# Neighbourhood attention: the reciprocal softmax sums of thirteen steps go through DRAM in place of a TensorE transpose

## The chip, the cores and the metric

The program runs on one core of one Trainium2 chip. The metric is the device time of one execution in microseconds (us), taken as the median of several runs. TensorE does matrix products and transposes into PSUM, VectorE and ScalarE do elementwise work, GpSimd moves small pieces and issues some transfers, and SyncE (SP) issues most transfers to and from DRAM. In the profile TensorE is PE (its weight loads are PEld), VectorE is DVE, ScalarE is ACT, GpSimd is POOL, and SPq is the queue of instructions of SyncE.

## The reference, cut to what matters

The reference is a network of two layers on 256 tokens of width 1024 with 256 context tokens, all in float32. The first layer mixes tokens with a retention, the second with a neighbourhood attention; an MLP follows each. The change lies in the neighbourhood attention (32 heads of 32 columns; the image is 4 rows of 64 columns). Every query sees the tokens in a window of its columns in all four rows, with a bias for each relative position, and all 256 context tokens:

```python
s_loc = jnp.einsum('bqhd,bikhd->bhqik', q_r, k_band).astype(jnp.float32) + bias
s_ctx = jnp.einsum('bqhd,blhd->bhql', q_r, k_c).astype(jnp.float32)
s = jnp.concatenate([s_loc.reshape(b, nh, GRID_W, band), s_ctx], axis=-1)
prob = jax.nn.softmax(s, axis=-1).astype(v.dtype)
p_loc = prob[..., :band].reshape(b, nh, GRID_W, kh, GRID_W)
return (jnp.einsum('bhqik,bikhd->bqhd', p_loc, v_band)
        + jnp.einsum('bhql,blhd->bqhd', prob[..., band:], v_c))
```

The kernel takes the exponentials first, multiplies them with the values, and divides by the sum of the exponentials at the end. The change concerns how the reciprocals of these sums reach the place where they are multiplied in.

## The kernel before, in words

The attention is cut into 16 steps, numbered n. Step n handles four heads (group `g = n // 2`) and half of the columns (`qt = n % 2`), that is 128 queries. A step consists of these functions:

- `scores(n)`: TensorE multiplies queries and keys into four PSUM banks, one for each head (`pqk`).
- `soften(n)`: for each head VectorE adds the bias and takes the minimum (the scores are kept negated), and ScalarE takes the exponential and adds up each row on the way. The sums of the four heads stand in a tile `sums[n]` of 128 queries x 4 heads, one of three buffers.
- `gather(n)`: GpSimd copies a few columns together and issues the loads of the bias of step n + 2.
- `invert(n)`: VectorE takes the reciprocal of the 4 sums of each query in place and copies it 32 times side by side into `rr` (128 queries x 128 columns: 32 equal columns for each head).
- `flip(n)`: TensorE transposes the exponentials in blocks of 128 x 128 into four PSUM banks (`ppt`, thirteen transposes), and ScalarE and VectorE copy them to SBUF (`pt`). At its end `flip_sums(n)` has TensorE transpose `rr` into the right part of a half of the bank `pav`, so that partition 32 j + d holds head j's reciprocals along the queries.
- `turned(n)`: ScalarE copies this transposed block from PSUM to the SBUF tile `rts[n]` (`rt` in the profile, one of two buffers).
- `attend(n)`: TensorE multiplies the transposed exponentials with the values into `pav`; VectorE multiplies the result with `rts[n]`; ScalarE and VectorE split the product into a high and a low part (`oTh`, `oTl`) for the output projection.

The steps are written out in a software pipeline. In iteration n of the loop over `STEPS` (n from 0 to 12) the scores and the softmax are those of step n + 2, the transposes those of step n + 1, and the attention product that of step n. The tuple of an iteration says how many units of weights are fetched and split at three places (`early` and `late` on either side of the softmax, `last` ahead of `attend`), and which projections run ahead of `flip` and behind `attend`. Between the steps stand the projections that make the keys, queries and values of later steps, and the first output projections. Before the loop stand `scores`, `soften` and `invert` of steps 0 and 1 and `flip(0)`; after the loop stand the last steps, by hand.

The order of the work on TensorE, ScalarE and VectorE is the order of the program text in this part of the kernel (an edge pins each instruction behind the one before it on its engine). On SP and GpSimd it is not: a planner that goes through the program at compile time puts their instructions in an order that respects all dependencies, and each of these queues then runs strictly in its order on the chip. SP issues the loads of weights: `fetch` loads a unit of 512 KB into one of four buffers (`raw`), ScalarE makes a rounded copy (`hi`), and VectorE the rest (`lo`, in `lows`); only when `lo` is made is the buffer free for the transfer four units later. Most helpers record their operations in one place, so that nearly every row of the profile has the line L84; rows are told apart by their tiles.

Of the kernel before, what the change touches and what calls it, by code (L numbers as in the profile page):

```python
# [10 lines left out]
F32 = mybir.dt.float32  # L11
# [6 lines left out]
P = 128  # L18
# [9 lines left out]
HD = 32  # L28
# [76 lines left out]
def kernel(  # L105
# [23 lines left out]
    pe, act, dve, pool, sp = (  # L129
        InOrder(tc, getattr(nc, e), e in PIN)  # L130
        for e in ("tensor", "scalar", "vector", "gpsimd", "sync")
    )
# [3 lines left out]
    smp = ec(tc.tile_pool(name="smp", bufs=4))  # L136
# [6 lines left out]
    dram = ec(tc.tile_pool(name="dram", bufs=1, space=DRAM))  # L143
# [8 lines left out]
    def nm(s):  # L152
        uid[0] += 1
        return f"{s}_{uid[0]}"

    def bank(s="ps"):
        return psp.tile([P, 512], F32, tag="ps", name=nm(s))
# [8 lines left out]
    def tsl(t):  # L166
        return slice(t * P, (t + 1) * P)
# [87 lines left out]
    def fetch(n, in_scratch=False, at=None):  # L255

        for src, k, ncol in specs[len(units) : len(units) + max(n, 0)]:
            raw = rawp.tile([P, k, ncol], F32, tag="raw", name=nm("raw"))
            sp.dma_start(out=raw[:], in_=src.rearrange("(k p) n -> p k n", p=P))
            if in_scratch or len(units) in scratch_units:  # L260
                hi, lo = Rows([scr("hi", F32R) for _ in range(k)]), Rows([scr("lo", F32R) for _ in range(k)])
                for i in range(k):
                    act.copy(out=hi[:, i, :], in_=raw[:, i, :])
                    pending.append((lo[:, i, :], raw[:, i, :], hi[:, i, :]))
                units.append((hi, lo))
                continue
            if at is None:
                hi = hip.tile([P, k, ncol], F32R, tag="hi", name=nm("hi"))
                lo = lop.tile([P, k, ncol], F32R, tag="lo", name=nm("lo"))
            else:  # L270
                both = slot(at, [P, 2, k, ncol], F32R, "hilo")
                hi, lo = both[:, 0], both[:, 1]
            act.copy(out=hi[:], in_=raw[:])
            pending.append((lo[:], raw[:], hi[:]))
            units.append((hi, lo))

    def lows(n=100, eng=None):
        for lo, raw, hi in pending[:n]:
            (eng or dve).tensor_sub(out=lo, in0=raw, in1=hi.bitcast(F32))
        del pending[:n]  # L280
# [591 lines left out]
    def part_v(k, a, b):  # L872
# [8 lines left out]
        out=lgn[:, 0], in_=ret_decay[0].rearrange("(o d) h -> o (d h)", o=1).broadcast_to([P, 8])  # L881
# [118 lines left out]
    for h in range(RH):  # L1000
# [102 lines left out]
        for t in range(4):  # L1103
            po = bank("po")
            scs = list(range(4)) if t < 2 else [2, 3]
            for i, sc in enumerate(scs):
# [9 lines left out]
                out=on, in0=po[:], scalar1=mv[:, 0:1], scalar2=r[:], op0=ALU.subtract, op1=ALU.mult  # L1116
# [312 lines left out]
    NS = 16  # L1429
# [70 lines left out]
    def v_part(half, t):  # L1500
        if t == 0:
            vu[0] = take(4, 0)
        ps = bank("pnv")
        for k in range(KC):
            wh, wl = vu[0][k // 2]
            mm3(ps[:], hs(k, t * P, (t + 1) * P), (wh[:, k % 2, :], wl[:, k % 2, :]), k == 0, k == KC - 1)
        act.copy(out=vtile(t, half), in_=ps[:])
# [28 lines left out]
    sums, rrs, Es, pts, pss = {}, {}, {}, {}, {}  # L1536

    def scores(n):

        g, qt = n // 2, n % 2  # L1540
        pss[n] = [bank("pqk") for _ in range(4)]
        q, k = q_of(g), kTs[g // 2][:, g % 2]
        for i, (a, b) in enumerate(((0, 0), (0, 1), (1, 0))):
            for j in range(4):
                js = slice(32 * j, 32 * j + 32)
                pe.matmul(
                    pss[n][j][:], lhsT=q[js, a, tsl(qt)], rhs=k[js, b, :], start=(i == 0), stop=(i == 2),
                    tile_position=(32 * j, 0),
                )

    def soften(n):

        mn = smp.tile([P, 4], F32, tag="mn", name=nm("mn"), bufs=3)
        sm = sums[n] = smp.tile([P, 4], F32, tag="sums", name=nm("sums"), bufs=3)
        for j in range(4):
            s = Es[n, j] = scr("s")
            dve.tensor_tensor_reduce(
                out=s[:].rearrange("p (a t) -> p a t", a=2),
                in0=pss[n][j][:].rearrange("p (a t) -> p a t", a=2),
                in1=bias_ap(n, j),  # L1560
                scale=1.0,
                scalar=3.0e38,
                op0=ALU.add,
                op1=ALU.min,
                accum_out=mn[:, j : j + 1],
            )
            act.activation(
                out=s[:], in_=s[:], func=AF.Exp, scale=-1.0, bias=mn[:, j : j + 1], accum_out=sm[:, j : j + 1]
            )
# [4 lines left out]
    def av_half(n):  # L1574
        return av[0][:, 256 * (n % 2) : 256 * (n % 2) + 256]

    def invert(n):

        rr = rrs[n] = smp.tile([P, 4, HD], F32, tag="rr", name=nm("rr"), bufs=1)
        dve.reciprocal(out=sums[n][:], in_=sums[n][:])  # L1580
        dve.tensor_copy(out=rr[:], in_=sums[n][:].unsqueeze(2).broadcast_to([P, 4, HD]))


# [4 lines left out]
    def pt_at(n, i):  # L1588
        return turns[n % 2][:, tsl(i)]

    def gather(n):

        o = 0 if n % 2 else P
        c0 = 24 if n % 2 else 0
        for j in range(4):
            pool.tensor_copy(
                out=pt_at(n, RAW)[:, 32 * j : 32 * j + 32].rearrange("p (r c) -> p r c", r=4),
                in_=Es[n, j][:, o : o + P].rearrange("p (r c) -> p r c", r=4)[:, :, c0 : c0 + 8],
            )
        if n + 2 < NS:  # L1600
            load_bias(n + 2)

    def flip(n, sums_too=True):
        for j in range(4):
            pp = bank("ppt")
            for i, kc in enumerate((n % 2, 2, 3)):
                pe.transpose(pp[:, tsl(i)], Es[n, j][:, tsl(kc)], ident)
            w = 3 * P
            if j == 3:
                pe.transpose(pp[:, tsl(3)], pt_at(n, RAW), ident)  # L1610
                w = 4 * P
            (dve.tensor_copy if j % 2 else act.copy)(
                out=turns[n % 2][:, 3 * j * P : 3 * j * P + w], in_=pp[:, :w]
            )
        if sums_too:
            flip_sums(n)

    def flip_sums(n):
        pe.transpose(av_half(n)[:, P:], rrs[n][:].rearrange("p h d -> p (h d)"), ident)

    oTs = [None]
    rts = {}

    def turned(n):

        rts[n] = smp.tile([P, P], F32, tag="rt", name=nm("rt"), bufs=2)
        act.copy(out=rts[n][:], in_=av_half(n)[:, P:])
# [30 lines left out]
    def rest_mm(half):  # L1658

        pr = bank("pnv")  # L1660
        sels = scr("sel")
        for qt in range(2):
            sel = sels[:, 32 * qt : 32 * qt + 32]
            pool.tensor_copy(
                out=sel.rearrange("p (r c) -> p r c", r=4),
                in_=ident.rearrange("p (r c) -> p r c", r=4)[:, :, 24 * qt : 24 * qt + 8],
            )
            v = vtile(1 - qt, half).rearrange("p (g j d) -> p j g d", g=4, j=4)
            for j in range(4):
                pe.matmul(  # L1670
                    pr[32 * j : 32 * j + 32, tsl(qt)], lhsT=sel, rhs=v[:, j], start=True, stop=True,
                    tile_position=(0, 32 * j),
                )
        return pr
# [96 lines left out]
    soften(1)  # L1771
    v_part(0, 1)
    invert(0)
    flip(0)
    rests = rest_mm(0)
    residual(1, xns[1], gb, dve)
    v_part(0, 2)
    rest_evac(rests)
    invert(1)
    v_part(0, 3)  # L1780

# [34 lines left out]
    def run(fs):  # L1816
        for f in fs:
            f()

    for n, (early, late, last, before, after) in enumerate(STEPS):  # L1820
        gather(n + 1)
        turned(n)
        fetch(early)
        lows(early)
        scores(n + 2)
        soften(n + 2)
        fetch(late)
        lows(late)
        run(before)
        flip(n + 1)  # L1830
        invert(n + 2)
        fetch(last)
        attend(n)
        run(after)

        lows(100 if n < len(STEPS) - 2 else len(STEPS) - 1 - n)


    n = NS - 1
    gather(n - 1)  # L1840
    turned(n - 2)
    flip(n - 1, False)
    fetch(1)
    attend(n - 2)
# [368 lines left out]
```

## Time and profile before

| | us |
|---|---|
| median of 3 runs (lowest to highest) | 1177.96 (1176.31 to 1180.05) |
| the profiled execution, its own time | 1176.32 |
| its span, first to last instruction | 1174.4 |
| TensorE busy in the span | 1161.8 |
| VectorE busy in the span | 848.4 |
| ScalarE busy in the span | 481.1 |
| GpSimd busy in the span | 235.1 |

The steps of the neighbourhood attention lie from about 819 us to 978 us after the start of the span. A row of the timeline names the start, the duration, the engine, the operation, the tile written and, behind the arrow, the tiles read, then how many instructions the row merges. What stands in brackets is the idle time of the engine ahead of it and what ended it. Matmuls overlap one another on TensorE, so that the distance from one start to the next, and not the duration, is what one costs.

### The profile page before, as it was taken

To read this page: it belongs to the slowest core of one execution; us is meant where nothing else is said; L and a number is where in the kernel's file an instruction comes from. 1 tells how busy PE (TensorE), PEld (TensorE's weight loads), DVE (VectorE), ACT (ScalarE), POOL (GpSimd) and SP (SyncE) were. 2 spreads that over 40 slices of the span, in tenths; PEclk is the share of its full clock that TensorE was granted. 3 is DMA by queue.
4 is the path that set the end of the run, shared out by engine and by line. 5 is a ranking of instruction groups with operands and counts; after the bars stand their busy time and mean duration, and the time that the engine had idled before them with its cause. 6 is when DMAs were issued, how large, how long until landed. Compare 5 with 4: busy or idle time off the path is not lost.

```text
span 1174.4 us, 17544 instructions
## 1 busy us (share of the span) xinstructions
PE 1161.8 (99%) x6687; PEld 980.7 (84%) x6687; DVE 848.4 (72%) x1361; ACT 481.1 (41%) x819; POOL 235.1 (20%) x418
## 2 busy tenths in 40 slices
PE   9999999999999999999999999999999999999997
PEld 6788888888888889888888888879778878999886
DVE  3786687777898787757777675578577589877456
ACT  3643332222323246441212333137466666756341
POOL 0102001010220241770312001223443430000001
PEclk9999999999999999999999999999999999999999
DMA  9943552544355426756556665646344335766760
GB/s 275 277 130 105 162 187 96 156 153 144 112 178 177 140 65 220 181 113 215 177 184 198 211 200 179 197 157 202 81 136 144 107 113 160 214 206 205 237 215 36
DMA packets 140115, 195.10 MB, mean 166 GB/s; under 512 B 9936, under 2 KB 81136, under 8 KB 140032
## 3 DMA queue, kind: packets, MB, share of 16 engines
q1 hardware_dynamic: 131904, 182.03, 49.8%
q0 software_dynamic: 6976, 9.39, 3.8%
q10 hardware_dynamic: 1152, 2.56, 0.7%
q8 instruction: 52, 0.85, 0.3%
q14 instruction: 31, 0.25, 0.1%
HBM read 189.12 MB, written 5.75 MB: 166 GB/s over the span
## 4 chain that ended last, share of the span: by engine, by line
PE 74%; DMA 12%; DVE 8%; issue 3%; ACT 2%; POOL 0%; DVEq 0%; ACTq 0%
PE p L84 23%; DMA rawa<-in_ada_w_dram 11%; PE pq L84 8%; PE pv L84 8%; PE pw L84 7%; PE pg L84 7%; PE pn L84 4%; DVE acc L84 4%; PE pnv L84 4%; PE po L84 3%; DVE lo L84 3%; PE pnw L84 1%; PE ppt L84 1%; PE pS L84 1%; PE pav L84 1%
## 5 line engine op out<-in xcount | busy, mean ns | idle before, releaser
L84 ACT CAST hi<-raw 128x1024 fp32r<-128x1024 f32 (+2 forms) x228 | 231.9, 1032 | 306.7 <-PE p L84 114.2
L84 DVE TENSOR_TENSOR lo<-raw,hi 128x1024 fp32r<-128x1024 f32 (+2 forms) x228 | 272.6, 1210 | 101.3 <-ACT hi L84 101.1
L84 PE MATMUL p<-hi,hid 128*128 128x512 f32 (+1 forms) x780 | 238.2, 386 | 0.0
L84 PEld LDWEIGHTS p<-hi,hid 128*128 128x128 f32 x780 | 145.7, 188 | 29.3
L84 PE MATMUL p<-hTl,hi 128*128 128x256 f32 (+1 forms) x512 | 165.9, 326 | 0.0
L84 PE MATMUL p<-hTh,lo 128*128 128x256 f32 (+1 forms) x512 | 165.9, 326 | 0.0
L84 PE MATMUL p<-hTh,hi 128*128 128x256 f32 (+1 forms) x512 | 162.6, 327 | 0.0
L84 PE MATMUL p<-lo,hid 128*128 128x512 f32 (+1 forms) x390 | 150.8, 387 | 2.1 <-DVE lo L84 2.1
L84 DVE SCALAR_TENSOR_TENSOR acc<-rawa,scol,acc 128x1024 f32<-128x1024 f32 x56 | 74.4, 1341 | 65.1 <-DMA rawa<-in_ada_w_dram 65.1
L84 PEld LDWEIGHTS p<-hTh,lo 128*128 128x128 f32 x512 | 96.3, 188 | 8.8
L84 PEld LDWEIGHTS p<-hTl,hi 128*128 128x128 f32 x512 | 96.4, 188 | 8.7
L84 PEld LDWEIGHTS p<-hTh,hi 128*128 128x128 f32 x512 | 94.3, 188 | 8.7
L84 PEld LDWEIGHTS p<-lo,hid 128*128 128x128 f32 x390 | 73.3, 188 | 17.9 <-DVE lo L84 3.2
L84 DVE SCALAR_TENSOR_TENSOR strips<-rawa,scol,strips 128x512 f32<-128x512 f32 x112 | 78.6, 764 | 0.0
L84 ACT CAST hid<-r 128x256 fp32r<-128x256 f32 (+1 forms) x64 | 31.9, 500 | 112.4 <-DVE r L84 112.3
L84 POOL TENSOR_TENSOR rstd<-rstd,misc 128x1 f32<-128x1 f32 x28 | 19.1, 684 | 216.5 <-DVE rstd L84 215.5
L84 ACT ACTIVATE s<-s,mn 128x512 f32<-128x512 f32 x64 | 45.5, 713 | 21.6 <-DVE mn L84 21.6
L84 PE MATMUL pw<-hi,oh 128*128 128x512 f32 x128 | 50.8, 397 | 0.0
L84 PE MATMUL pg<-hi,hTh 128*128 128x512 f32 x128 | 50.6, 395 | 0.0
L84 PE MATMUL pw<-hi,ol 128*128 128x512 f32 x128 | 50.0, 390 | 0.0
L84 PE MATMUL pg<-hi,hTl 128*128 128x512 f32 x128 | 49.9, 390 | 0.0
L84 PE MATMUL pw<-lo,oh 128*128 128x512 f32 x128 | 49.8, 389 | 0.0
(241 smaller groups left out, 2275.2 us busy)
## 6 DMA issues: line engine op xcount, KB each, us to landing
raw<-in_mlp_w_dram SPq DMA_DIRECT2D x128, 512.0 KB, 4.5
rawa<-in_ada_w_dram SPq DMA_DIRECT2D x80, 512.0 KB, 3.9
raw<-in_ret_w_in_dram SPq DMA_DIRECT2D x42, 512.0 KB, 4.0
raw<-in_nat_w_in_dram SPq DMA_DIRECT2D x24, 512.0 KB, 4.1
rawq<-in_ada_w_dram SPq DMA_DIRECT2D x16, 512.0 KB, 6.0
raw<-in_ret_w_o_dram SPq DMA_DIRECT2D x16, 512.0 KB, 3.5
bias<-rpb_rows POOLq DMA_DIRECT2D x32, 128.0 KB, 2.9
raw<-in_nat_w_o_dram SPq DMA_DIRECT2D x8, 512.0 KB, 3.7
```

The lines of the kernel that those rows point to most:

```text
L84: r = f(*args, **kwargs)
```

## The change

The reciprocals of steps 0 to 12 are no longer copied 32 times, transposed and copied out of PSUM. VectorE still takes the reciprocal in `sums[n]`. `store_sums(n)` then has SP write the 128 x 4 block to DRAM with heads outermost (each head's 128 reciprocals in a row), and `load_sums(n)` has SP read it back into `rts[n]`, each head's row of 512 bytes to 32 partitions. Steps 13 to 15 go on as before.

```diff
+    rsums = dram.tile([NS, 4, P], F32, tag="rsums", name="rsums")
+    BY_DMA = range(13)
+
+    def store_sums(n):
+        if n in BY_DMA:
+            sp.dma_start(out=rsums[n].rearrange("j q -> q j"), in_=sums[n][:])
+
+    def load_sums(n):
+        rts[n] = smp.tile([P, P], F32, tag="rt", name=nm("rt"), bufs=2)
+        row = rsums[n]
+        sp.dma_start(out=rts[n][:], in_=bass.AP(row.tensor, row.offset, [[P, 4], [0, HD], [1, P]]))
+
     def invert(n):
 
+        dve.reciprocal(out=sums[n][:], in_=sums[n][:])
+        if n in BY_DMA:
+            return
         rr = rrs[n] = smp.tile([P, 4, HD], F32, tag="rr", name=nm("rr"), bufs=1)
-        dve.reciprocal(out=sums[n][:], in_=sums[n][:])
         dve.tensor_copy(out=rr[:], in_=sums[n][:].unsqueeze(2).broadcast_to([P, 4, HD]))
...
-        if sums_too:
+        if sums_too and n not in BY_DMA:
             flip_sums(n)
...
     invert(0)
+    store_sums(0)
     flip(0)
...
     for n, (early, late, last, before, after) in enumerate(STEPS):
         gather(n + 1)
-        turned(n)
+        store_sums(n + 1)
+        load_sums(n)
         fetch(early)
```

## The prediction

> **What bounds the kernel now.** I read the page first: each engine's busy time in us and as a share of the span.
>
> ```profile
> PE 1161.8 (99%) x6687; PEld 980.7 (84%) x6687; DVE 848.4 (72%) x1361; ACT 481.1 (41%) x819; POOL 235.1 (20%) x418
> ```
>
> TensorE has work in 99% of the span. An average says nothing of one stage, so next comes the view by stretches: the loop up to its ninth iteration, the rest of the attention, and all that follows.
>
> ```profile
> 838.00:926.00 88.00, 88.00 (x741) 72.09 (x743) 57.79 (x157) 54.21 (x135) 36.87 (x90) 1.00 0.39 112
> 926.00:978.00 52.00, 51.87 (x486) 41.94 (x479) 41.20 (x99) 35.58 (x84) 15.81 (x40) 1.00 0.48 147
> 978.00:1174.00 196.00, 188.72 (x1264) 173.02 (x1262) 135.48 (x195) 96.60 (x155) 6.47 (x6) 0.99 0.56 180
> ```
>
> After the length stand the busy times of PE, PEld, DVE, ACT and POOL, then the granted clock, the DMA share and GB/s. PE is full in the stretches that the change touches, at a granted clock of 1.00. DVE (57.79 of 88) and ACT (54.21 of 88) have a third to spare. Since matmuls overlap and a busy PE may still be held up, I read the waits of the weight loads from 838 to 978, us in total, times and longest: the largest row and the one on the tile that goes away:
>
> ```profile
> PEld pqk L84 <- issue: 1.1, 5, 0.4
> ...
> PEld pav L84 <- DVE rr L84: 0.2, 1, 0.2
> ```
>
> and the largest from 978 to the end:
>
> ```profile
> PEld p1t L84 <- ACT hi L84: 0.3, 1, 0.3
> ```
>
> The largest is 1.1 us in 140 us, in pieces of at most 0.4, and "issue" means that PE waited for no other engine. So TensorE's own list of instructions sets the end: what leaves it shortens the run by its pitch, and what leaves DVE or ACT is worth nothing until one of them holds PE up.
>
> **The change part by part.** First what goes. The tiles `rr` and `rt` give count and duration (minimum/median/maximum in ns):
>
> ```profile
> L84 DVE COPY rr<-sums x16: 226/227/295, 826.8 to 972.6; 128x128 f32<-128x128 f32 x16
> L84 PE MATMUL pav<-cst,rr x16: 272/273/328, 830.6 to 972.9; 128*128 128x128 f32 x16
> L84 ACT COPY rt<-pav x16: 259/261/272, 843.1 to 973.3; 128x128 f32<-128x128 f32 x16
> ```
>
> Thirteen of the 16 of each go. The 273 ns of the transpose are not its cost, because matmuls overlap; the timeline of PE has the pitch:
>
> ```profile
> 850.45 0.27 PE L84 MATMUL pav<-cst,rr 128*128 128x128 f32 x1
> 850.55 0.39 PE L84 MATMUL pav<-pt,G 128*128 128x128 f32 x2
> ```
>
> The transpose of `rr` starts at 850.45 and the next matmul at 850.55: 0.10 us. The chain that ended last (here followed back inside the attention's stretch) checks it, since it has an `attend` with and one without that transpose ahead:
>
> ```profile
> 850.61 1.12 PE pav L84 x27
> ...
> 970.41 1.01 PE pav L84 x26
> ```
>
> 27 matmuls took 1.12 us and 26 took 1.01: 0.11 us. So 13 x 0.11 = **1.4 us** leave the path (1.3 by the lower pitch).
>
> The 13 copies on DVE (13 x 0.227 = 3.0 us) and on ACT (13 x 0.261 = 3.4 us) leave engines that are not the bound. I count them at nothing; the first rival prices that. The reciprocal stays.
>
> Now what comes: on SP's queue 13 stores of 128 x 4 x 4 bytes = 2 KB and 13 loads of 128 rows of 512 bytes = 64 KB, and a wait of the multiplication in `attend(n)` for the load. Queued behind that multiplication on DVE are the low part `oTl` and the bias additions of `soften(n + 3)`; ACT's `oTh` and its exponentials wait for these. How long may a round trip take? From DVE's timeline:
>
> ```profile
> 941.25 0.17 DVE L84 RECIPROCAL sums<-sums 128x4 f32<-128x4 f32 x1
> ...
> 941.66 0.28 DVE L84 TENSOR_TENSOR rt<-pav,rt 128x128 f32<-128x128 f32 x1
> ...
> 947.93 0.29 DVE L84 TENSOR_TENSOR rt<-pav,rt 128x128 f32<-128x128 f32 x1
> ...
> 958.15 0.28 DVE L84 TENSOR_TENSOR rt<-pav,rt 128x128 f32<-128x128 f32 x1
> ```
>
> The three multiplications are those of steps 9, 10 and 11, and the reciprocal is that of step 11: `invert(n + 2)` stands ahead of `attend(n)`. From 941.25 to 958.15 there are **16.9 us**, the shortest such window of the steps that change. No transfer of this form is in the trace. The nearest rows of the page's list (KB each, median us to landing), and the extremes of the tiles `rpb_rows` and `raw`:
>
> ```profile
> raw<-in_nat_w_in_dram SPq DMA_DIRECT2D x24, 512.0 KB, 4.1
> gb<-lns SPq DMA_DIRECT2D x6, 512.0 KB, 5.6
> rpb_rows<-rpb_neg POOLq DMA_DIRECT2D x49, 14.0 KB, 3.4
> ```
>
> ```profile
> DMA to landing us min/median/max: 2.0/3.0/6.6
> ```
>
> ```profile
> DMA to landing us min/median/max: 3.4/4.3/7.7
> ```
>
> For the store the nearest is the write of short runs to DRAM, 3.4 us (bounds 2.0 and 6.6). For the load it is `gb<-lns`, also rows of DRAM repeated over partitions, 5.6 us (bounds 2.0 and 7.7). I take 3.4 + 5.6 = 9.0 us; the bounds are 4.0 and 14.3. Both ends are below 16.9, so the wait costs nothing, if SP issues the load as soon as the store has landed. `rt` has two buffers, so the load of step n also waits for `oTl` of step n - 2, about 1.3 us after the reciprocal: inside the store's time. If the planner instead keeps the load at its place in the text, the start of iteration n, it has one iteration: 947.93 - 941.66 = 6.3 us in the shortest, 958.15 - 947.93 = 10.2 in the next. 5.6 is still inside, 7.7 would be 1.4 late in two or three iterations.
>
> What the transfers are moved past on SP: the fetches. They may wait up to one landing (7.7) behind a load that waits for its store.
>
> ```profile
> 858.77 1.50 SPq L84 DMA_DIRECT2D raw<-in_nat_w_in_dram  x2
> ```
>
> ```profile
> 876.38 1.03 ACT L84 CAST hi<-raw 128x1024 fp32r<-128x1024 f32 x1
> ```
>
> The first of these two transfers fills the buffer of the unit that ACT casts at 876.38 (four buffers, in turn): 17.6 us after its issue, less 4.1 to land, leaves 13.5. That cover hides it. SP itself stands waiting most of this time:
>
> ```profile
> SPq L84 <- DVE lo L84: 139.8, 19, 30.4
> ```
>
> 139.8 us of 820 to 980, so 26 issues (the 1.50 above for two with a gap bound one at 0.75: 20 us) find room. The `sums` buffer is written again by `soften(n + 3)`, which on ACT comes after `attend(n)`; for that the load has landed, so the store is done. Added traffic is 13 x 66 KB = 0.86 MB at a DMA share of 0.39: nothing.
>
> The sum, against the profiled execution: 1176.32 - 1.4 = 1174.9. It stands 1.64 below the median of the runs, 1177.96, and I predict the median: 1177.96 - 1.4 = **1176.6 us**. Nothing is late next: PE goes from the last transpose of the exponentials straight to `attend`, whose inputs were copied an iteration before.
>
> **The rivals.** *DVE's relief counts too.* Where PE waits for PSUM banks that DVE and ACT empty, an earlier copy is an earlier PE.
>
> ```profile
> 869.91 0.97 PE L84 MATMUL pqk<-kT,qT 32*128 32x512 f32 x12
> ...
> 888.71 1.60 PE L84 MATMUL pqk<-kT,qT 32*128 32x512 f32 x12
> ```
>
> The scores took 0.97 us in one iteration and 1.60 in another, so such waits exist. If each of the 13 copies of 0.227 moved PE up: 1.4 + 3.0 = 4.4 us, 1173.6. Against it: the second row is the longest of its kind, and PE's waits above add up to little.
>
> *The load is late* (the other side). SP runs strictly in order, and the planner may put the load of step n behind a fetch that waits for a `lo` of the same iteration. In DVE's timeline:
>
> ```profile
> 857.52 2.36 DVE L84 TENSOR_TENSOR lo<-raw,hi 128x1024 fp32r<-128x1024 f32 x2 [2.17 <-ACT hi L84]
> ...
> 861.87 0.28 DVE L84 TENSOR_TENSOR rt<-pav,rt 128x128 f32<-128x128 f32 x1
> ```
>
> The last `lo` ends at 859.88 and the multiplication is at 861.87, so a load issued there that takes 4.1 is 2.1 late, with 5.6 it is 3.6 late. The slack behind it, from ACT's timeline in the next iteration:
>
> ```profile
> 863.58 0.73 ACT L84 ACTIVATE s<-s,mn 128x512 f32<-128x512 f32 x1 [0.92 <-DVE mn L84]
> ...
> 868.78 0.85 ACT L84 COPY pt<-ppt 128x384 f32<-128x384 f32 x2
> ```
>
> ACT waits for DVE at 863.58 and then has no pause to 869.63, when it frees the bank that the scores at 869.91 need some 0.2 us into their run: about 0.5 us of slack. So PE loses 2.1 - 0.5 = 1.6, in the six iterations (1 to 5 and 9) whose `late` is not zero: 9.6 - 1.4 = 8.2 us slower, 1186; with 5.6 it is 1195. It decides against the change once the load lands over 0.7 us after the multiplication's present start in those six (6 x 0.2 uses up the gain), and measurably from 1.3. For it: SP stands at the head of its queue for up to 30.4 us. Against it: a fetch waits for `lo` of four units earlier, which is made later than the point where the load is ready.
>
> *The store is slow.* It writes 512 single elements; a transfer of the row of 3.4 us has, by the code, 224 runs (32 heads x 7 rows). In proportion the slowest, 6.6, becomes 15.1, and with 5.6 for the load 20.7: 3.8 late, 3.3 beyond the slack. A late step widens the two windows that span it, so about one in three is late, four times 3.3 less 1.4: 1190. Against it: by the median, 3.4 becomes 7.8 and 13.4 is inside the window. The Trainium skill, page "DMA: Bandwidth & Descriptors", section "Rules for kernel authors", speaks against this store: a strided last dimension lowers to one descriptor per element, and it advises rearranging so that it is contiguous. By that rule the 512 pieces hold, and the time is the one just given or, by the median, no loss; no run here shows it yet.
>
> *It does nothing.* The pitch saved may return as a longer pause at the change of shape, since pauses of 0.2 to 0.4 stand there already: 1178.0.
>
> **How the numbers follow.** Chances: forecast 0.68, nothing 0.08, DVE's relief 0.08, late load 0.11, slow store 0.05. A measurement of this kernel can tell about 0.3%, 3.5 us, from no change. Forecast and nothing lie within: same 0.76. DVE's relief is faster: 0.08. The last two are slower: 0.16. The forecast's own range is 1174.5 to 1179.5, the spread of three runs (3.7 us) about it. For 8 in 10 I reach down past DVE's relief, 1172.5, and up into mild forms of the late load, 1183.
>
> **What would show it.** In the changed kernel the rows `pav<-cst,rr`, `rr<-sums` and `rt<-pav` of ACT count 3, not 16; `attend` in the chain has 26 matmuls in 1.01 us; each of the thirteen iterations is 0.11 shorter and all after 978 keeps its length. Stores land in 2.0 to 6.6, loads in 2.0 to 7.7, and no row has DVE waiting for a transfer into `rt`. The prediction is wrong if DVE idles ahead of that multiplication with `rsums` as the cause, if PE waits grow above the 1.1 us of now, or if SP waits for a store while ACT waits for `raw`.

## The result, and the profile after

The changed kernel takes **1206.97 us** (median), the kernel before, on the same chip, 1176.31. The ratio is 1.0268 with a 95% interval of 1.0247 to 1.0288: slower by about 31 us, where 1176.6 us and no measurable change were predicted. One of its five executions took 2996.73 us; why is not known, and the ratio leaves it out. The profiled execution of the changed kernel took 1206.01 us, its span is 1204.2; that is 29.7 us more than the 1176.32 of the profiled execution before.

The first part of its page, busy time and share of the span by engine:

```profile
PE 1171.8 (97%) x6674; PEld 984.0 (82%) x6674; DVE 845.9 (70%) x1348; ACT 478.0 (40%) x806; POOL 234.5 (19%) x418
```

The counts are as planned: 13 fewer on PE, DVE and ACT. But PE is busy for 97% of the span, not 99%: it now waits. The view by stretches, with the columns as before, says where:

```profile
838.00:926.00 88.00, 82.22 (x616) 64.87 (x614) 47.28 (x119) 43.01 (x101) 28.04 (x68) 0.96 0.70 108
926.00:978.00 52.00, 40.26 (x330) 31.49 (x329) 25.66 (x68) 24.41 (x59) 16.95 (x42) 0.90 0.49 80
```

PE was full in both stretches before (88.00 and 51.87 us). Now it gets through 616 + 330 = 946 matmuls in these 140 us, in place of 741 + 486 = 1227; its granted clock is 0.96 and 0.90 in place of 1.00, and the DMA share of the first stretch is 0.70 in place of 0.39, although fewer bytes move (108 GB/s against 112). The tile `rt`, for SP's loads and for the copies of the three steps that go on as before:

```profile
L84 SPq DMA_DIRECT2D rt<-rsums x13: 534/535/630, 837.6 to 990.0; - x13
L84 ACT COPY rt<-pav x3: 259/266/267, 994.4 to 1002.8; 128x128 f32<-128x128 f32 x3
```

The last copy starts at 1002.8, before at 973.3: 29.5 of the 29.7 us are lost by then. The loss lies in the thirteen steps and nowhere else. Who waits, by the view of the waits from 820 to 1010 (us in total, times, longest):

```profile
ACT oTh L84 <- DVE rt L84: 48.1, 13, 8.0
DVE rt L84 <- DMA rt<-rsums: 37.6, 7, 8.8
...
ACT hi L84 <- DMA raw<-in_nat_w_o_dram: 3.4, 1, 3.4
POOL G L84 <- DMA bias<-rpb_rows: 3.2, 3, 1.7
```

DVE waits 37.6 us for loads of `rt`; ACT waits behind DVE; the two small rows are transfers that the change does not touch and that are late nevertheless. Read DVE's timeline for the first multiplications:

```profile
861.48 0.26 DVE L84 TENSOR_TENSOR rt<-pav,rt 128x128 f32<-128x128 f32 x1
...
871.01 0.17 DVE L84 RECIPROCAL sums<-sums 128x4 f32<-128x4 f32 x1
871.09 0.26 DVE L84 TENSOR_TENSOR rt<-pav,rt 128x128 f32<-128x128 f32 x1
...
884.20 0.29 DVE L84 TENSOR_TENSOR rt<-pav,rt 128x128 f32<-128x128 f32 x1 [4.57 <-DMA rt<-rsums]
```

The multiplications are those of steps 1, 2 and 3; the reciprocal is that of step 4. Step 1 is at most 0.4 us from its place before (861.87); from step 3 on the load is late. The cause is in the row of the tile `rsums`, time from issue to landing (minimum, median, maximum), and in what SP waits for from 820 to 1000:

```profile
DMA to landing us min/median/max: 10.7/11.0/11.3
```

```profile
SPq L84 <- DMA rsums<-sums: 118.8, 12, 12.6
SPq L84 <- DVE lo L84: 11.2, 4, 4.8
```

A store of 2 KB lands in 11.0 us. The prediction took 3.4, with 6.6 as the bound. SP, which stood waiting for `lo` before, now waits for stores. Its own timeline shows what this does to the order of the queue:

```profile
863.61 0.53 SPq L84 DMA_DIRECT2D rt<-rsums  x1
864.24 1.82 SPq L84 DMA_DIRECT2D raw<-in_nat_w_in_dram  x2
866.15 0.42 SPq L84 DMA_DIRECT2D rsums<-sums  x1
879.28 0.54 SPq L84 DMA_DIRECT2D rt<-rsums  x1
879.91 0.94 SPq L84 DMA_DIRECT2D raw<-in_nat_w_in_dram  x2
880.91 0.61 SPq L84 DMA_DIRECT2D rsums<-sums  x1
892.78 0.53 SPq L84 DMA_DIRECT2D rt<-rsums  x1
```

The order is store, load (waiting at the head for the store to land), fetches, next store. This turn takes 879.28 to 892.78, 13.5 us (the thirteen loads, 837.6 to 990.0, are 12.7 apart on average), more than the 9.6 us that lie between the first two multiplications above. The store at 880.91 is that of step 4, whose reciprocal was taken at 871.01: it was issued 9.9 us later, behind step 3's load and two fetches.

So two questions are left: why does a store of 2 KB take 11 us, and how does that become 31?

### The profile page after: what moved, and what is told of

Read it like the earlier page. It is cut to its first block, busy times and chain, and to the rows that moved or that the text cites. A ratio compares the mean times of both kernels' runs of the same rounds, so it can differ in the third digit from the quotient of the medians.

```text
span 1204.2 us, 17568 instructions
## 1 busy us (share of the span) xinstructions
PE 1171.8 (97%) x6674; PEld 984.0 (82%) x6674; DVE 845.9 (70%) x1348; ACT 478.0 (40%) x806; POOL 234.5 (19%) x418
## 5 line engine op out<-in xcount | busy, mean ns | idle before, releaser
L84 DVE TENSOR_TENSOR lo<-raw,hi 128x1024 fp32r<-128x1024 f32 (+2 forms) x228 | 272.8, 1211 | 101.5 <-ACT hi L84 101.3
L84 PEld LDWEIGHTS p<-hi,hid 128*128 128x128 f32 x780 | 145.7, 188 | 29.5
L84 PE MATMUL pn<-hTh,hi 128*128 128x256 f32 (+1 forms) x144 | 47.6, 331 | 5.6 <-ACT hi L84 5.6
```

The lines of the kernel that those rows point to most:

```text
L84: r = f(*args, **kwargs)
```

## The experiments

The edits are against the changed kernel unless something else is said.

### What there was to gain, and whether three steps do harm

`e_ceiling`: no store, no load, no transpose; `rt` is set to one.

```diff
-            sp.dma_start(out=rsums[n].rearrange("j q -> q j"), in_=sums[n][:])
+            pass
...
-        sp.dma_start(out=rts[n][:], in_=bass.AP(row.tensor, row.offset, ...))
+        pool.memset(rts[n][:], 1.0)
```

> Left out: the reciprocals of steps 0 to 12 are neither transposed nor sent through DRAM; GpSimd fills rt with ones. What remains is the removal alone. Theory (TensorE is the bound, 13 transposes at a pitch of 0.11 us): 1.4 us below the kernel before, ratio 0.9988. Rival (VectorE's and ScalarE's relief counts too): 4.4 us below, ratio 0.9963.

Measured: 1172.91 us against 1175.55, ratio 0.9981 (0.9967 to 0.9995), about 2.2 us less. The gain part of the prediction (1.4 us) lies in the interval (0.6 to 3.9 us). That is about all that a transfer in place of the transpose could have brought.

`e_first3`: the round trip for the first three steps alone, the transpose for the others.

```diff
-    BY_DMA = range(13)
+    BY_DMA = range(3)
...
-        load_sums(n)
+        load_sums(n) if n in BY_DMA else turned(n)
```

> The round trip through DRAM for steps 0 to 2 alone, the others by transpose. Theory (SP's queue takes one round trip of some 12 us for each step while an iteration takes 9, so SP falls behind step by step and the first loads are still in time): no loss, ratio 0.999 to 1.001, VectorE never waits for rt. Rival (each round trip has a price of its own, by disturbing the other transfers): 3/13 of 31 us, 7 us more, ratio 1.006.

Measured: ratio 0.9998 (0.9987 to 1.0010). The three stores are just as slow:

```profile
DMA to landing us min/median/max: 10.1/11.3/12.5
```

No row of its waits has DVE waiting for `rt`. A slow store by itself is inside the window for a step or two; what hurts is that it comes every 9.6 us and takes more than that.

### Why the store is slow

Two runs keep the load and change only where the store puts its values. `e_runs16` writes each query's four values side by side, 128 pieces of 16 bytes. `e_spread` writes 512 single elements as before, but each 64 bytes from the next (the block was filled with ones at the start).

```diff
 # e_runs16
+            sp.dma_start(out=rsums[n].rearrange("j q -> (j q)").rearrange("(q j) -> q j", j=4), in_=sums[n][:])
 # e_spread
+    rsums = dram.tile([16, P, 4, 16], F32, tag="rsums", name="rsums")
...
+            sp.dma_start(out=rsums[n][:, :, 0], in_=sums[n][:])
```

> The store writes each query's four reciprocals side by side, 128 pieces of 16 bytes in place of 512 of 4, and the load reads the same 2 KB in the same form as the changed kernel, so the values arrive in another order. Theory (the store is late because of its single elements): it lands in about 3 us, SP waits about 3 us for each and VectorE never; ratio 0.999. If the latency goes with the number of pieces: 11/4 = 2.8 us plus a fixed part of 2, nearly the same. Rival (a write to DRAM that is read back takes about 10 us whatever its form): unchanged, ratio 1.027.

> The store still writes 512 single elements of 4 bytes, but 64 bytes apart (32 KB in place of 2 KB); two transfers fill the area with ones far ahead, and the load reads rows of 512 bytes of it, so the values are not the reciprocals. If the number of pieces makes the store slow: it lands in about 11 us again, ratio 1.027. If it is that many pieces fall on the same bytes of DRAM (sixteen to each 64), it lands in about 3 us, ratio about 0.999.

Measured: 0.9979 (0.9964 to 0.9994) and 0.9985 (0.9970 to 0.9999). Both keep all that the ceiling has to give, round trip included. The landing of the store in `e_runs16` and, second, in `e_spread`:

```profile
DMA to landing us min/median/max: 2.9/2.9/3.1
```

```profile
DMA to landing us min/median/max: 2.4/3.0/3.6
```

So the number of elements alone does not make the store slow: 512 of them land in 3.0 us, as fast as 128 pieces. What differs is that in the changed kernel they stand close together: sixteen go into the same 64 bytes. Four runs with other distances follow: 16 bytes (four in 64), 8 bytes (eight in 64), 512 bytes (none shared), and the changed kernel's own order with its four rows 8704 bytes apart.

```diff
 # e_pitch16, e_pitch8, e_pitch512: D = 4, 2, 128
+    rsums = dram.tile([16, P, 4, D], F32, tag="rsums", name="rsums")
+            sp.dma_start(out=rsums[n][:, :, 0], in_=sums[n][:])
 # e_rows
+    rsums = dram.tile([NS, 4, 17 * P], F32, tag="rsums", name="rsums")
+            sp.dma_start(out=rsums[n][:, :P].rearrange("j q -> q j"), in_=sums[n][:])
+        ... [[17 * P, 4], [0, HD], [1, P]]
```

> 512 single elements of 4 bytes, 16 bytes apart (8 KB for a step; the area is filled with ones ahead, the values that the load reads are not the reciprocals). Four of them fall on each 64 bytes, in place of sixteen in the changed kernel and one at a pitch of 64. If the landing goes with the writes to the same 64 bytes: 3 + 8 x 3/15, about 4.6 us. If only writes from several queries' transfers to the same bytes hold each other up (here the four are one query's): 3 us. If neighbouring 512 bytes are what counts: 8 us or more.

> As the run with the elements 16 bytes apart, but 8 bytes apart (eight in 64 bytes; other values, so the attention of these steps is divided by something else). Store landing so far, by elements in 64 bytes: 3.0 us for one, 5.1 for four, 11.0 for sixteen. Theory 'same 64 bytes': the elements of one 64-byte piece are written one after another, about 0.53 us for each further one (8.0 us over 15 further ones), while different pieces go side by side: 3.0 + 7 x 0.53 = 6.7 us, by the step from one to four (0.7 each) 7.9. Theory 'number of elements' gives 3.0, as for the other runs of 512. Theory 'size of the region' (these runs wrote into 32, 8 and 2 KB): between 5.1 and 11.0 as well; the other run of this pair tells it apart.

> 512 single elements, each 512 bytes from the next (256 KB a store; other values, as in the other runs with a distance). Theory 'same 64 bytes': nothing is shared, so the store lands in about 3.0 us, as at 64 bytes apart, and SP waits about 2.5 a store. Theory 'distance': addresses that differ by a large power of two get in one another's way, as the fours 1024 bytes apart did (7.8 of waiting a store against 3.4); with none shared I expect more than 5 us of waiting a store.

> The changed kernel with the four rows of a step 8704 bytes apart in place of 512: sixteen elements still share each 64 bytes, in the same order, but the step covers 27 KB. Theory 'same 64 bytes': landing 11 us and about 1204 us as in the changed kernel. Theory 'small region' (2 KB lie in one place of DRAM): the four rows go side by side, landing at 5 us or less and about 1175.

The landings of these four, in the same order:

```profile
DMA to landing us min/median/max: 3.8/5.1/5.4
```

```profile
DMA to landing us min/median/max: 4.4/7.9/9.8
```

```profile
DMA to landing us min/median/max: 2.2/2.6/3.5
```

```profile
DMA to landing us min/median/max: 9.9/10.9/12.4
```

| elements in the same 64 bytes | 1 (64 or 512 bytes apart) | 4 | 8 | 16 (rows together or 8704 apart) |
|---|---|---|---|---|
| median landing, us | 3.0, 2.6 | 5.1 | 7.9 | 11.0, 10.9 |

The closer the single elements stand, the longer the store takes: counted by elements in 64 bytes, the landing grows by 8.0/15 = 0.53 us for each further one (0.4 to 0.7 between neighbours in the table). `e_rows` covers 27 KB where the changed kernel covers 2 and is as slow (one run, 1210.27 us against 1179.66 before), so the size of the region isn't it. Three things stay open. No distance between 16 and 64 bytes was run, so the 64 is only how I count and not a measured boundary. `e_runs16` has four pieces in each 64 bytes as well and landed in 2.9 us where `e_pitch16` took 5.1; whether its longer pieces or their smaller number (128) spare it was not separated. And with sixteen, all neighbouring elements come from different queries, while at 8 bytes eight neighbours are those of two queries and at 16 bytes four are those of one; what this order adds was not separated.

The one run of `e_pitch16` took 1171.8 us, that of `e_pitch8` 1173.16 (1174.59 before), that of `e_pitch512` 1178.62 (1179.66 before). In `e_pitch8` 7.9 us still fit: DVE waited 0.4 us for `rt` in all.

The stretch from 838 to 926 in `e_spread` and, second, in `e_pitch8` shows it from the side of the DMA engines (the last three numbers are the granted clock, the DMA share and GB/s):

```profile
838.00:926.00 88.00, 88.00 (x763) 72.38 (x762) 56.99 (x145) 54.24 (x126) 36.83 (x90) 1.00 0.47 122
```

```profile
838.00:926.00 88.00, 88.00 (x762) 72.41 (x761) 56.98 (x144) 54.18 (x126) 36.87 (x90) 1.00 0.67 122
```

The same 122 GB/s, and the same 512 elements in each store, keep the DMA engines busy for 0.67 of the time in place of 0.47.

`e_far16` and `e_far1088` put the groups of four 1024 and 1088 bytes from one another in place of 64.

```diff
 # e_far16: W = 256; e_far1088: W = 272
+    rsums = dram.tile([16, P, W], F32, tag="rsums", name="rsums")
+            sp.dma_start(out=rsums[n][:, 0:16:4], in_=sums[n][:])
```

> 512 elements, four in each 64 bytes, 16 bytes apart, as in the run before with that distance, but each group of four stands 1024 bytes from the next, so that the store covers 128 KB in place of 8 (other values, as there). Theory 'same 64 bytes': the landing stays at about 5.1 us (4.6 to 5.8). Theory 'size of the region': it falls to 3.0 us or less, the landing of the run that covered 32 KB.

> The fours of 16 bytes distance again, but 1088 bytes from one four to the next (17 times 64; at 1024 SP waited 7.8 us a store, at 64 it was 3.4; other values, as there). Theory 'same 64 bytes' with a bad power of two: back to about 3.4 of waiting a store, 5 us to land. Theory 'the farther, the slower' (each four opens another place in DRAM): 7.8 again.

`e_far16` came out against both theories: SP's waits for its stores in it and, second, in `e_far1088`, and the landing in `e_far1088`:

```profile
SPq L84 <- DMA rsums<-sums: 101.5, 13, 11.6
```

```profile
SPq L84 <- DMA rsums<-sums: 42.0, 13, 5.1
```

```profile
DMA to landing us min/median/max: 3.0/3.7/4.5
```

At 1024 bytes SP waits 101.5/13 = 7.8 us a store, and the one run took 1188.09 us (1174.59 before). At 1088 bytes it waits 42.0/13 = 3.2 us a store, much as at 64 (44.4/13 = 3.4), the store lands in 3.7 us, and the run took 1170.99 (1179.66 before). By the wait the first theory of `e_far1088` holds, by the landing (5 expected) the store is faster than it said. Four close elements therefore land in 3.7 to 5.1 us, and a distance of 1024 bytes between the groups makes it worse; single elements 512 bytes apart do not suffer. So how closely the elements of a group stand is not all that counts. Why 1024 is bad is left open. It bears on no step of the change, whose groups of sixteen follow one another.

### How 11 us become 31

Two runs take the slow transfers off one queue. `e_store_act` issues the stores from ScalarE's queue, `e_load_act` the loads; the other half stays on SP.

```diff
 # e_store_act
-            sp.dma_start(out=rsums[n].rearrange("j q -> q j"), in_=sums[n][:])
+            act.dma_start(out=rsums[n].rearrange("j q -> q j"), in_=sums[n][:])
 # e_load_act
-        sp.dma_start(out=rts[n][:], in_=bass.AP(...))
+        act.dma_start(out=rts[n][:], in_=bass.AP(...))
```

> The stores of 512 single elements to neighbouring addresses stay, but ScalarE's queue issues them (at the place of store_sums in the program), so on SP a store no longer stands behind the load that waits for the store before. Theory (the loss comes from SP taking one round trip for each step): stores overlap, the load of step n lands some 6.4 us after iteration n begins where 9 are there; ratio 1.000 to 1.004, VectorE waits in the short iterations at most. Rival (the slow writes cost by themselves, by holding up the other transfers): ratio stays above 1.015.

> As in the changed kernel, but ScalarE's queue issues the loads, at the start of iteration n; the stores stay on SP, where nothing waits for their landing any more. Theory: a store is issued right after its reciprocal, some 10 us ahead of iteration n, and lands in 8 to 13, so ScalarE waits 0 to 3 us for it in an iteration and the load lands 5 us later, before the multiplication in most; weights are no longer late. Ratio 0.999 to 1.008. Rival (slow writes hold up the other transfers): above 1.015.

Measured: 1.0202 (1.0180 to 1.0225) and 1.0196 (1.0166 to 1.0225). My first theory, that SP's order alone turns the landing into the loss, fell: some 8 us come back (2.68% less 2.0% of 1176) and some 23 remain. In `e_store_act` SP is not free, since the loads still wait at its head for the stores (132.8 us from 820 to 1000). In `e_load_act` SP no longer waits for a store at all, and yet, from 820 to 1010:

```profile
ACT oTh L84 <- DVE rt L84: 42.2, 13, 7.0
DVE rt L84 <- DMA rt<-rsums: 30.7, 8, 7.6
```

One of these loads and its multiplication, with the stores around them, in the timeline of `e_load_act`:

```profile
872.09 0.37 SPq L84 DMA_DIRECT2D rsums<-sums  x1
...
875.79 0.51 ACTq L84 DMA_DIRECT2D rt<-rsums  x1
...
885.08 0.29 DVE L84 TENSOR_TENSOR rt<-pav,rt 128x128 f32<-128x128 f32 x1 [1.13 <-DMA rt<-rsums]
```

The load of 64 KB is issued at 875.79 while the store of 872.09 is on its way, and releases DVE at 885.08: 9.3 us. It doesn't wait for its own store, which is that of step 3 and was issued at 861.14. The eight loads that DVE waits for in this run release it 9.3 to 12.7 us after their issue, and each is issued only at the start of its own iteration, right behind `oTh` of the step before: it has one step, not 16.9 us. In the changed kernel, where a load is issued when a store has just landed, the load of 879.28 released DVE at 884.20, 4.9 us (six of the seven that DVE waits for take 3.7 to 6.3). That points to slow transfers while a slow store is open. To price that by itself, `e_stores_only` adds the thirteen stores to the kernel *before*; nobody reads them.

```diff
 # against the kernel before
+    rsums = dram.tile([NS, 4, P], F32, tag="rsums", name="rsums")
+            sp.dma_start(out=rsums[n].rearrange("j q -> q j"), in_=sums[n][:])
...
+    store_sums(0)
...
+        store_sums(n + 1)
```

`e_loads_free` is the changed kernel with loads that read a block of ones, so that they don't wait for the store.

```diff
-        row = rsums[n]
+        row = ones[n]
```

> The kernel before with the 13 slow stores of the changed kernel added on SP. Nobody reads what they write; the transposes stay, so no step waits for a round trip. Theory 'waiting': the 29 us or so of the changed kernel come from the chain store, landing, load, landing, multiplication. Without readers, SP issues each store at once, the weights may still land in about 9 us in place of 4.3, inside their cover of 13.5, and the time is that of before, 0.998 to 1.004. Theory 'crowding': a store of this form holds up every other transfer of the core for some 5 us, and the late weights and biases alone cost most of what remained with the stores on ACT's queue (24 us): 1.013 to 1.022. In both, the stores should land in 10 to 11 us, as in the changed kernel.

> The changed kernel, with its 13 slow stores and 13 loads, but each load reads a block of ones that was written at the start of the program, so that it need not wait for its store (the attention is not divided by the sums in these steps). Theory 'waiting': the loads are issued as soon as their buffer is free, DVE no longer waits for rt, and the time is that of the kernel without the transposes, 0.996 to 1.003. Theory 'crowding': the loads still land late beside the stores (8 us or more, which is inside their window of 16.9), and the weights and biases are as late as before: 1.013 to 1.022, with ACT waiting for raw and POOL for bias, not DVE for rt.

Measured: 1.0065 (1.0042 to 1.0087) and 1.0063 (1.0040 to 1.0085). Neither theory's range holds them; they lie between. The stores alone cost 7.6 us with nobody waiting for them. The transfers from 826 to 950 in `e_stores_only` (KB each, median us to landing):

```profile
raw<-in_nat_w_in_dram SPq DMA_DIRECT2D x9, 512.0 KB, 9.8
raw<-in_nat_w_o_dram SPq DMA_DIRECT2D x6, 512.0 KB, 12.2
bias<-rpb_rows POOLq DMA_DIRECT2D x20, 128.0 KB, 7.2
```

and the same rows before:

```profile
raw<-in_nat_w_in_dram SPq DMA_DIRECT2D x9, 512.0 KB, 4.3
bias<-rpb_rows POOLq DMA_DIRECT2D x24, 128.0 KB, 2.9
raw<-in_nat_w_o_dram SPq DMA_DIRECT2D x6, 512.0 KB, 4.1
```

Twice to three times as long, beside 2 KB each. The DMA share from 838 to 926 is 0.82, against 0.39 before, at 109 GB/s against 112. It shows as waits for biases, none of which was among the rows of 1.1 us and more before (from 820 to 1010):

```profile
POOL G L84 <- DMA bias<-rpb_rows: 12.0, 6, 3.7
...
POOL bias L84 <- DMA bias<-rpb_rows: 4.0, 2, 2.3
...
DVE s L84 <- DMA bias<-rpb_rows: 1.9, 1, 1.9
```

In `e_spread`, with as many elements but none in the same 64 bytes, both are about as before:

```profile
raw<-in_nat_w_in_dram SPq DMA_DIRECT2D x9, 512.0 KB, 4.0
...
bias<-rpb_rows POOLq DMA_DIRECT2D x24, 128.0 KB, 3.2
```

So the crowding, too, comes with the packing and not with the number of elements.

Put together, counted from the ceiling (-2.2 us) and in us of 1176: crowding alone takes it to +7.4 (`e_loads_free`, whose loads are issued as soon as their buffer is free, some two steps before they are needed), a round trip with one half on ScalarE's queue to +23 or +24 (`e_load_act`, `e_store_act`), and both halves on SP to +31. What lies between +7.4 and +23 is the multiplication's wait for its load: in `e_load_act` because the load is issued one step ahead and is slow, in `e_store_act` because it also stands on SP until its store has landed. These are steps of one ladder, not independent costs, since each makes the others worse, and the two runs in the middle change the place of a transfer in the order together with its queue. How much of each is the lower granted clock (0.90 in the stretch of 926 to 978) was not separated.

### A store that shares nothing it needn't

`e_blocks` turns the reciprocals on VectorE in blocks of 32 x 32 first, so that the store writes runs of 128 bytes (16 KB with the columns of ones, in place of 2).

```diff
+    rsums = dram.tile([NS, 32, 4, 32], F32, tag="rsums", name="rsums")
+    rrt = smp.tile([P, 4, HD], F32, tag="rr", name=nm("rr"), bufs=1)
+    pool.memset(rrt[:, 3, :], 1.0)
...
+            sp.dma_start(out=rsums[n].rearrange("j b c -> b j c"), in_=rrt[:, n % 3, :])
...
+            dve.reciprocal(out=rrt[:, 3, 0:4], in_=sums[n][:])
+            dve.transpose(out=rrt[:, n % 3, :], in_=rrt[:, 3, :])
```

> The whole computation, with the store in runs of 128 bytes: VectorE turns the reciprocals in blocks of 32 x 32 (a tile of 128 x 32 whose other 28 columns are ones) and SP stores its 128 rows of 32 values, each head's reciprocals in a row of 512 bytes as before. Theory (what is slow is many small writes to the same 64 bytes of DRAM): the store lands in about 3 us, VectorE never waits for rt, and the run comes out like the one in which nothing replaces the transposes: 1.4 to 2.2 us below the kernel before, ratio 0.998 to 0.999. Rival (the block transpose on VectorE delays the exponentials, or the store is still slow): ratio 1.002 or more.

Measured: 1174.78 us against 1174.07, ratio 0.9998 (0.9985 to 1.0011): the whole loss is gone. The ratio lies above the 0.998 to 0.999 that was expected, and the interval reaches into that range. SP waits 23.3/12 = 1.9 us for a store, no row of its waits has DVE waiting for a load of `rt`, and its stretch from 838 reads as before the change:

```profile
838.00:926.00 88.00, 88.00 (x759) 72.02 (x758) 58.75 (x153) 54.09 (x126) 36.73 (x90) 1.00 0.45 124
```

It is no faster than the kernel before either, and with a ceiling of 0.2% there is little to win by any version of this idea.

## Why the prediction was wrong

*What bounds the kernel: right.* TensorE is the bound, and what leaves its list shortens the run by about its pitch: 1.4 us forecast, 2.2 (0.6 to 3.9) measured at the ceiling. The 4.4 us that DVE's relief would have made of it lie just outside.

*The step that failed is the term "3.4 us for the store, bounds 2.0 and 6.6".* It was taken from `rpb_rows<-rpb_neg`, a write of short runs. That row writes runs; this store writes single elements, sixteen into the same 64 bytes, and took 11.0, because they stand so close. With the predicted load of 5.6 the sum is 16.6, just inside the 16.9 of the shortest window: with the size alone mended, the forecast would still have stood. Two further steps were needed.

*"So the wait costs nothing, if SP issues the load as soon as the store has landed."* It does, but I followed one step through the queue, not two: the store of step n + 1 stands behind the load of step n, which waits at the head. The right measure of a wait in an in-order queue that comes back every step is the step (9.6 us), not the window of one value (16.9). A turn took 13.5 us, and the load was late from step 3 on. Moving one half to ScalarE's queue brought back some 8 us; since that moves the transfer in the order too, what this part costs by itself stays open.

*"Added traffic ... nothing."* Counted in bytes, yes; but with stores of this kind the landing of `raw` and `bias` became two to three times as long (4.1, 4.3 and 2.9 us became 12.2, 9.8 and 7.2 in `e_stores_only`). This part costs 7.4 to 7.6 us with nobody waiting, and through slower loads more.

*The rivals.* "The store is slow" had the right place and a chance of 0.05. Its reason was the number of elements, its price 1190; the 11.0 us measured lie between its 7.8 and 15.1, and with a load of 5.6 they would still have been inside its window. The Trainium skill, page "DMA: Bandwidth & Descriptors", section "Rules for kernel authors", has a strided last dimension lower to one descriptor per element and advises against it. The packets of all transfers from 826 to 950, in the changed kernel and, second, before, bear the first half out:

```profile
DMA packets 13034, 11.26 MB, mean 91 GB/s; under 512 B 6428, under 2 KB 10140, under 8 KB 13023
```

```profile
DMA packets 8451, 14.35 MB, mean 116 GB/s; under 512 B 1394, under 2 KB 3954, under 8 KB 8438
```

6428 of under 512 bytes against 1394 are some 500 more for each of the ten stores in that stretch. But the price does not come with them, since 512 single elements apart land in 2.6 to 3.0 us. Following the advice would have saved the 31 us (as `e_runs16` and `e_blocks` show), but the count of descriptors that this section gives as its reason is not what cost them. "The load is late" had the place on SP right and the wrong thing ahead of the load: not a fetch that waits for `lo`, but the load's own store, and the next store behind the load.

*The signs named beforehand.* All three that would make it wrong came: DVE idles before the multiplication with `rsums` as the cause (37.6 us), PE's waits grew, and ACT waits for `raw` (3.4 us). The largest waits of PE's weight loads from 838 to 1010, where 1.1 was the largest before:

```profile
PEld pn L84 <- ACT hi L84: 5.8, 1, 5.8
PEld ppt L84 <- DVE mn L84: 4.5, 8, 2.5
PEld pqk L84 <- ACT pt L84: 3.1, 3, 2.7
```

## What to carry to other kernels

Before a small store to DRAM replaces work on an engine, ask how closely its single elements stand; keep them in runs (16 bytes were enough here) or apart (64 bytes were enough), and turn the block on an engine first where the order forbids both. Price a round trip through a queue by the period at which it returns, with the next step's store behind this step's load, and not by the time until one value is needed. And a ceiling run, which leaves out old and new work alike, is cheap: here it would have said at once that 0.2% was all there was to win.

## What the runs showed of the hardware

- In stores of 512 single elements of 4 bytes to DRAM, the landing rises as the elements stand closer: 2.6 us at 512 bytes from one to the next, 3.0 at 64, 5.1 at 16, 7.9 at 8, and 11.0 where sixteen fill each 64 bytes. 128 pieces of 16 bytes that follow one another landed in 2.9. Why close elements cost is open.
- With such stores in the kernel (sixteen elements in each 64 bytes), other transfers, those that GpSimd issues too, took two to three times as long to land: 512 KB 9.8 and 12.2 us in place of 4.3 and 4.1, 128 KB 7.2 in place of 2.9.
- With groups of four, SP waited 3.4 us for each store at 64 bytes from group to group, 3.2 at 1088, and 7.8 at 1024. Why is open.
- Where PE waited, its granted clock was lower: 0.90 in the stretch in which it was busy for 40.26 of 52 us, 0.93 in the same stretch of `e_store_act` (46.26 us), 1.00 before (51.87 us). What the lower clock adds to a wait was not measured.
